# Scores of a differential attention as three 64-row products, two maps in the two halves of the array

## The chip, the cores and the metric

The kernel runs on one core of a Trainium2 chip. The metric is the device time of one execution in microseconds (us). Before the change it is 1723.46 us, the median of three runs (1720.41 to 1724.44).

## The reference: what is computed

One decoder layer over 2048 tokens of width 1024. A normalised input is projected once; half of the columns feed four heads of a gated delta rule, the other half four heads of differential attention; both outputs are concatenated and go through an output projection back to the residual stream. The change lies in the attention's scores. Each head has two maps `c`, with 64 columns of q and of k each:

```python
q = rmsnorm(q.reshape(b, t, DF_HEADS, 2, DF_HEAD_QK), q_gain) * (DF_HEAD_QK ** -0.5)
k = rmsnorm(k.reshape(b, t, DF_HEADS, 2, DF_HEAD_QK), k_gain)
...
s = jnp.einsum('bqhcd,bkhcd->bhcqk', q_blk, k).astype(jnp.float32)
mask = key_pos[None, :] <= q_pos[:, None]
p = jax.nn.softmax(jnp.where(mask, s, neg), axis=-1)
wts = p[:, :, 0] - lam * p[:, :, 1]
```

## The kernel before, in words

Products on TensorE use the rounded type `F32R`. Where more precision is wanted, a number is kept as a rounded part ("hi") and the rest ("lo"). So every q and k of the attention lies in DRAM twice, as hi and lo (`qst_d[h]`, `kst_d[h]`: 2 x 128 x 2048; the 128 are the 64 columns of map 0, then the 64 of map 1).

The program has two halves in time. The first 1100 us or so are the input projection (tiles `pnat`, `pct`) and the delta rule. Then, from about 1143 us to 1664 us, come the attention's scores, mixed with its values and with the output projection (`outp`). The attention goes through (head, group) pairs in the list `SEQ`: 4 heads x 8 groups of 256 query tokens, each group as two query blocks `qt` of 128. For each block, `scores` walks over the keys up to the diagonal in pieces of 512 (the last of 128 to 512), 160 pieces with two maps each in `m = 0, 1`:

- a PSUM bank `sp` is taken, one of three (`SPB = 3`);
- two products fill it, one with q-hi and one with q-lo as stationary matrix. `load_group` puts q twice into the 128 rows of `qs`, and `load_k` puts k-hi in rows 0 to 63 and k-lo in rows 64 to 127 of a tile per map. So one product of 128 rows gives q times (k-hi + k-lo);
- on the last piece a third product of 128 columns (`identr` and `cmask`) adds the causal mask;
- VectorE takes the row maximum (L940), ScalarE the exponential (L942) with it, and the bank is free again.

`values` then scales both maps, combines them (L994), transposes the weights on TensorE (`wtp`, evacuated at L1000 and L1002), and multiplies with v (`oT`, `pv`). `epilogue` normalises. `out_half` is the output projection.

TensorE works in program order. That order is set twice: by the generators (`abreast` interleaves scores, values and epilogue; `mingle` puts the output projection between), and then by the framework's scheduler, which reorders by its own estimate (`schedule_with_timeline_sim=True`). The `Recorder` class makes every product one source line: L113 (matmul) and L116 (transpose). Tiles tell them apart. The DMAs are issued on SyncE: k at L892, qs at L907.

In the changed file two lines stand ahead, so L113 is L115 there, L116 is L118, and so on.

One more product matters for the prediction. `ccp` at the start of the program transposes 60 rows of constants; it and the changed scores are the products that use 64 of the array's 128 rows as a tile of their own (the first transpose, `ngp`, uses 32, and `gctp` uses all rows and 32 columns).

Of the kernel before, what the change touches and what calls it, by code (L numbers as in the profile page):

```python
# [11 lines left out]
F32R = mybir.dt.float32r  # L12
# [4 lines left out]
P = 128  # L17
# [4 lines left out]
HALF = 1024  # L22
G = 512
# [25 lines left out]
QSB = 3  # L49
# [6 lines left out]
KB = (2, 2)  # L56
LAGX = 5
SPB = 3
# [5 lines left out]
WOR = 2  # L64
EXB = 14
WTB = 4

LEVELS = [1, 2, 4, 8, 16, 32, 64]

# [8 lines left out]
def f(ap):  # L78
    return ap.bitcast(F32)
# [3 lines left out]
def hybrid_kernel(  # L83
# [21 lines left out]
    V, A, PL, SY = nc.vector, nc.scalar, nc.gpsimd, nc.sync  # L105
# [55 lines left out]
    def bc(ap, shape):  # L161
        return ap.broadcast_to(shape)


    kst_d = [dram.tile([2, P, T], F32, name=f"kst_d{h}") for h in range(H)]
    qst_d = [dram.tile([2, P, T], F32, name=f"qst_d{h}") for h in range(H)]
# [708 lines left out]
    def bank(tag, name, bufs, shape=S4):  # L875
        return psa.tile(shape, F32, tag=tag, name=name, bufs=bufs)
# [8 lines left out]
    kst, vv = {}, {}  # L885

    def load_k(h, hf):
        cs = slice(hf * HALF, (hf + 1) * HALF)
        for m in range(2):
            k = kp.tile([P, HALF], F32R, tag=f"k{hf}", name=f"k{hf}", bufs=2 * KB[hf])  # L890
            for q in range(2):
                SY.dma_start(out=f(k[64 * q : 64 * q + 64]), in_=kst_d[h][q, 64 * m : 64 * m + 64, cs])  # L892
            kst[h, m, hf] = k

    def load_v(h, hf):
        cs = slice(hf * HALF, (hf + 1) * HALF)
# [4 lines left out]
    def load_group(h, g):  # L901
        c = dict(h=h, g=g, wt={})
        cs = slice(2 * g * P, 2 * (g + 1) * P)
        c["qs"] = qs = kp.tile([P, 2, 2, 2 * P], F32R, tag="qs", name="qs", bufs=QSB)
        for r in range(2):
            for m in range(2):
                SY.dma_start(  # L907
                    out=f(qs[64 * r : 64 * r + 64, m]),
                    in_=qst_d[h][:, 64 * m : 64 * m + 64, cs].rearrange("a p t -> p a t"),
                )  # L910
        c["zz"] = zz = kp.tile([P, 2 * P], F32, tag="azz", name="azz", bufs=QSB)
        SY.dma_start(out=zz, in_=z_d[h][:, cs])
        c["rs"] = kp.tile([P, 2, 2], F32, tag="rs", name="rs", bufs=5)
        return c

    def scores(c, qt):

        n = (2 * c["g"] + qt + 1) * P
        npc = (n + G - 1) // G
        nm = ap.tile([P, 2, 4], F32, tag="nm", name="nm", bufs=3)  # L920
        ss = ap.tile([P, 2, 4], F32, tag="ss", name="ss", bufs=3)
        c["ex"] = ex = {}
        for pi in range(npc):
            k0 = pi * G
            w = min(G, n - k0)
            for m in range(2):
                sp = bank("sp", "sp", SPB, [P, G])
                diag = pi == npc - 1
                for a in range(2):
                    PE.matmul(  # L930
                        sp[:, :w],
                        lhsT=c["qs"][:, m, a, qt * P : (qt + 1) * P],
                        rhs=kst[c["h"], m, k0 // HALF][:, k0 % HALF : k0 % HALF + w],
                        start=(a == 0),
                        stop=(a == 1 and not diag),
                    )
                if diag:
                    PE.matmul(sp[:, w - P : w], lhsT=identr, rhs=cmask, start=False, stop=True)
                mx = nm[:, m, pi : pi + 1]
                V.tensor_reduce(mx, sp[:, :w], axis=AX.X, op=ALU.max, negate=True)  # L940
                e = ap.tile([P, G], F32, tag="ex", name="ex", bufs=EXB)
                A.activation(e[:, :w], sp[:, :w], AF.Exp, bias=mx, accum_out=ss[:, m, pi : pi + 1])  # L942
                ex[m, pi] = e
                yield
        al = ap.tile([P, 2, 4], F32, tag="al", name="al", bufs=3)
        S3 = [P, 2, npc]
        if npc > 1:
            nmin = ap.tile([P, 2], F32, tag="nmin", name="nmin", bufs=3)
            V.tensor_reduce(nmin, nm[:, :, :npc], axis=AX.X, op=ALU.min)
            V.tensor_tensor(al[:, :, :npc], bc(nmin.unsqueeze(2), S3), nm[:, :, :npc], op=ALU.subtract)  # L950
            A.activation(al[:, :, :npc], al[:, :, :npc], AF.Exp)  # L951
        else:
            V.memset(al[:, :, 0:1], 1.0)
        c["al"], c["ss"] = al, ss
# [17 lines left out]
    def values(c, qt):  # L972
# [7 lines left out]
        for pi in range(npc):  # L980
            w = min(G, n - pi * G)
            nbk = w // P
            if pi not in wt:
                wt[pi] = ap.tile([P, 4, 2 * P], F32, tag="wt", name="wt", bufs=WTB)
            e0, e1 = ex[0, pi], ex[1, pi]
# [83 lines left out]
    def prefetch(i, j):  # L1069

        for n, (h, g) in enumerate(SEQ[:i]):
            for hf in range(g // 4 + 1):

                if n >= len(groups) and h not in have[hf][-KB[hf] :]:
                    have[hf].append(h)
                    load_k(h, hf)
                    if ap:
                        load_v(h, hf)
        for h, g in SEQ[len(groups) : j]:
            groups.append(load_group(h, g))  # L1080

    def attention():
        before = after = None
        for hf in range(2):
            for h in have[hf]:
                load_v(h, hf)
        for i in range(len(SEQ)):
            prefetch(i + 1, i + 1)
            prefetch(i + AHEAD, i + GA)
            for qt in range(2):  # L1090
                c = dict(groups[i])
                npc = (2 * c["g"] + qt + 4) // 4
                yield from abreast((scores(c, qt), 2 * npc), before, after)
                after = (epilogue(before[2]), 3) if before and qt == 0 else None
                before = (values(c, qt), (2 * npc + 1 if qt else npc + 1), c)
        scored[0] = True
        yield from abreast(before, after)
        yield from epilogue(before[2])
# [184 lines left out]
```

## Time and profile before

| | us |
|---|---|
| runs | 1720.41, 1723.46, 1724.44 |
| the profiled execution | 1718.26 |
| its span, first to last instruction | 1716.1 |
| TensorE busy in the span | 1622.8 (95%) |
| VectorE busy | 1066.1 (62%) |
| ScalarE busy | 751.6 (44%) |
| mean granted TensorE clock | 0.984 |

The profiled execution is 5.2 us under the median of the runs. Between its span and its time lie 2.2 us. A matmul's end in the trace is modelled; how fast TensorE goes through a row of products is read from the distance of their starts. "PEld" is the load of the stationary matrix, which normally runs beside the product before it.

### The profile page before, as it was taken

Reading aid. Unit: us, or ns where it says so; the run is one execution under the profiler, and the core shown is the slowest. Engines: PE = TensorE matmul, PEld = TensorE weight load, DVE = VectorE, ACT = ScalarE, POOL = GpSimd, SP = SyncE. Lnnn points to the kernel's source line nnn. Section 1 sums busy time; section 2 is a strip of 40 time slices with the busy share of each in tenths; the row PEclk is TensorE's granted clock in tenths of the full one; section 3 lists DMA queues with packets and bytes.
Section 4 is the critical chain, followed back from the end, with each engine's and each line's share of the span. In section 5 each row is a group of like instructions: output and inputs, shape, how many; then the busy total and the mean of one; then the engine's idle time right before and its main releaser. Section 6 shows DMA issues by size and latency. Waiting matters only on the chain.

```text
span 1716.1 us, 28068 instructions
## 1 busy us (share of the span) xinstructions
PE 1622.8 (95%) x9900; PEld 1414.1 (82%) x9900; DVE 1066.1 (62%) x2435; ACT 751.6 (44%) x2153; POOL 680.7 (40%) x789
## 2 busy tenths in 40 slices
PE   6999999999999899999999999989999989999987
PEld 5788899898988888889989898868777867778766
DVE  4765655645444486556573643337888778888772
ACT  5333333333334343433342333236777656565530
POOL 3454374253242256327344144022334354343432
PEclk9999999999999899999999999999999999999998
DMA  8232244233234341323313232596743364543343
GB/s 175 62 93 74 44 90 101 62 93 56 62 99 103 71 125 61 83 66 72 114 43 106 37 62 75 139 285 201 198 139 117 121 192 149 167 143 101 119 151 135
DMA packets 186969, 188.16 MB, mean 110 GB/s; under 512 B 12242, under 2 KB 142412, under 8 KB 186828
## 3 DMA queue, kind: packets, MB, share of 16 engines
q1 hardware_dynamic: 186556, 185.78, 39.5%
q8 instruction: 78, 1.28, 0.3%
q0 software_dynamic: 272, 0.59, 0.2%
q14 instruction: 63, 0.52, 0.1%
HBM read 124.42 MB, written 61.90 MB: 109 GB/s over the span
## 4 chain that ended last, share of the span: by engine, by line
PE 75%; DVE 8%; DMA 7%; ACT 4%; POOL 3%; issue 2%; SPq 1%; DVEq 0%; POOLq 0%; ACTq 0%
PE pct L113 24%; PE pnat L113 15%; PE outp L113 7%; PE oT L113 6%; PE sp L113 5%; PE wtp L116 2%; DVE nm L940 2%; PE xp L113 2%; DVE ex L994 2%; PE np L113 2%; PE tp L116 2%; DMA wr_fqk<-in_w_in_dram 2%; PE gqp L113 2%; ACT ex L942 1%; PE op L113 1%
## 5 line engine op out<-in xcount | busy, mean ns | idle before, releaser
L942 ACT ACTIVATE ex<-sp,nm 128x512 f32<-128x512 f32 (+3 forms) x320 | 198.5, 625 | 94.2 <-DVE nm L940 82.8
L113 PE MATMUL outp<-wo,mt 128*128 128x512 f32 x720 | 202.4, 414 | 5.2 <-ACT wo L1119 2.1
L940 DVE TENSOR_REDUCE nm<-sp 128x1 f32<-128x512 f32 (+3 forms) x320 | 186.3, 600 | 27.2 <-PE sp L113 25.6
L113 PE MATMUL sp<-k,qs 128*128 128x512 f32 (+3 forms) x640 | 184.4, 392 | 19.0 <-ACT ex L942 18.1
L113 PE MATMUL pnat<-wh_fqk,xh 128*128 128x256 f32 (+1 forms) x512 | 152.9, 300 | 16.0 <-ACT wh_fqk L336 8.8
L113 PEld LDWEIGHTS outp<-wo,mt 128*128 128x128 f32 x720 | 131.4, 193 | 31.4 <-ACT xr L1193 3.0
L113 PE MATMUL pnat<-wl_fqk,xh 128*128 128x256 f32 (+1 forms) x512 | 151.4, 297 | 1.6 <-POOL wl_fqk L337 1.6
L113 PE MATMUL pnat<-wh_fqk,xl 128*128 128x256 f32 (+1 forms) x512 | 150.1, 295 | 0.0
L113 PEld LDWEIGHTS sp<-k,qs 128*128 128x128 f32 x640 | 106.6, 190 | 49.6 <-ACT ex L942 37.5
L113 PE MATMUL oT<-wt,v 128*128 128x256 f32 (+1 forms) x576 | 132.7, 375 | 0.0
L528 DVE SCALAR_TENSOR_TENSOR cy<-craw,cc,cy 128x512 f32<-128x512 f32 x144 | 122.8, 853 | 3.3
L990 POOL TENSOR_SCALAR ex<-ex,al 128x512 f32<-128x512 f32 (+3 forms) x140 | 98.2, 716 | 61.4 <-ACT al L951 60.9
L113 PEld LDWEIGHTS oT<-wt,v 128*128 128x128 f32 x576 | 109.0, 193 | 16.2 <-ACT wt L1000 0.5
L994 DVE SCALAR_TENSOR_TENSOR ex<-ex,cf 128x512 f32<-128x512 f32 (+3 forms) x160 | 112.7, 743 | 12.9 <-ACT cf L969 10.0
L662 ACT CAST u_TT<-tp 128x512 fp32r<-128x512 f32 x112 | 65.5, 587 | 117.7 <-PE tp L116 117.6
L113 PEld LDWEIGHTS pnat<-wh_fqk,xh 128*128 128x128 f32 x512 | 99.7, 195 | 18.3 <-ACT wh_fqk L336 10.4
L113 PE MATMUL pct<-xh,wh_dvz 128*128 128x512 f32 x256 | 103.8, 406 | 0.0
L113 PE MATMUL pct<-xh,wh_dqk 128*128 128x512 f32 x256 | 103.5, 405 | 0.0
L113 PE MATMUL pct<-xl,wh_dvz 128*128 128x512 f32 x256 | 103.1, 403 | 0.0
L113 PE MATMUL pct<-xh,wl_dvz 128*128 128x512 f32 x256 | 103.0, 403 | 0.0
L113 PEld LDWEIGHTS pnat<-wl_fqk,xh 128*128 128x128 f32 x512 | 100.0, 195 | 3.3 <-POOL wl_fqk L337 3.0
L113 PE MATMUL pct<-xl,wh_dqk 128*128 128x512 f32 x256 | 102.6, 401 | 0.0
(271 smaller groups left out, 4179.4 us busy)
## 6 DMA issues: line engine op xcount, KB each, us to landing
qs<-qst_d SPq DMA_DIRECT2D x128, 128.0 KB, 3.1
mt<-mx_d SPq DMA_DIRECT2D x48, 256.0 KB, 4.0
k<-kst_d SPq DMA_DIRECT2D x40, 256.0 KB, 5.4
wr_dqk<-in_w_in_dram SPq DMA_DIRECT2D x32, 256.0 KB, 5.7
wr_dvz<-in_w_in_dram SPq DMA_DIRECT2D x32, 256.0 KB, 5.7
qst_d<-qkhl SPq DMA_DIRECT2D x16, 512.0 KB, 2.8
kst_d<-qkhl SPq DMA_DIRECT2D x16, 512.0 KB, 3.4
part_d<-xr SPq DMA_DIRECT2D x32, 256.0 KB, 3.7
```

What stands on the lines that cost most here:

```text
L113: last[0] = nc.tensor.matmul(*a, **k)
L116: last[0] = nc.tensor.transpose(*a, **k)
L528: V.scalar_tensor_tensor(y, raw[:, j : j + G], convc[:, j, idx : idx + 1], y, op0=ALU.mult, op1=ALU.add)
L662: A.copy(TT, f(tp))
L940: V.tensor_reduce(mx, sp[:, :w], axis=AX.X, op=ALU.max, negate=True)
L942: A.activation(e[:, :w], sp[:, :w], AF.Exp, bias=mx, accum_out=ss[:, m, pi : pi + 1])
L990: PL.tensor_scalar(e0[:, :w], e0[:, :w], al[:, 0, pi : pi + 1], 1.0, op0=ALU.mult, op1=ALU.mult)
L994: V.scalar_tensor_tensor(e1[:, :w], e1[:, :w], cf[:, pi : pi + 1], e0[:, :w], op0=ALU.mult, op1=ALU.add)
```

## The change

The scores' tiles hold q and k once, hi and lo side by side in the free dimension, with map 0 in rows 0 to 63 and map 1 in rows 64 to 127. For each piece two `sp` banks are taken together, and three terms (hi·hi, hi·lo, lo·hi; lo·lo is left out) are written as products of 64 rows, alternating between the maps. The mask, the maximum and the exponential follow for both maps. Four DMAs for k of a head's half become two, four for qs become one.

```diff
+TERMS = ((0, 0), (0, 1), (1, 0))
     def load_k(h, hf):
         cs = slice(hf * HALF, (hf + 1) * HALF)
-        for m in range(2):
-            k = kp.tile([P, HALF], F32R, tag=f"k{hf}", name=f"k{hf}", bufs=2 * KB[hf])
-            for q in range(2):
-                SY.dma_start(out=f(k[64 * q : 64 * q + 64]), in_=kst_d[h][q, 64 * m : 64 * m + 64, cs])
-            kst[h, m, hf] = k
+        k = kp.tile([P, 2, HALF], F32R, tag=f"k{hf}", name=f"k{hf}", bufs=KB[hf])
+        for q in range(2):
+            SY.dma_start(out=f(k[:, q]), in_=kst_d[h][q, :, cs])
+        kst[h, hf] = k
...
-        c["qs"] = qs = kp.tile([P, 2, 2, 2 * P], F32R, tag="qs", name="qs", bufs=QSB)
-        for r in range(2):
-            for m in range(2):
-                SY.dma_start(
-                    out=f(qs[64 * r : 64 * r + 64, m]),
-                    in_=qst_d[h][:, 64 * m : 64 * m + 64, cs].rearrange("a p t -> p a t"),
-                )
+        c["qs"] = qs = kp.tile([P, 2, 2 * P], F32R, tag="qs", name="qs", bufs=QSB)
+        SY.dma_start(out=f(qs), in_=qst_d[h][:, :, cs].rearrange("a p t -> p a t"))
...
-            for m in range(2):
-                sp = bank("sp", "sp", SPB, [P, G])
-                diag = pi == npc - 1
-                for a in range(2):
+            sps = [bank("sp", "sp", SPB, [P, G]) for m in range(2)]
+            diag = pi == npc - 1
+
+            for qa, ka in TERMS:
+                for m in range(2):
+                    rows = slice(64 * m, 64 * m + 64)
                     PE.matmul(
-                        sp[:, :w],
-                        lhsT=c["qs"][:, m, a, qt * P : (qt + 1) * P],
-                        rhs=kst[c["h"], m, k0 // HALF][:, k0 % HALF : k0 % HALF + w],
-                        start=(a == 0),
-                        stop=(a == 1 and not diag),
+                        sps[m][:, :w],
+                        lhsT=c["qs"][rows, qa, qt * P : (qt + 1) * P],
+                        rhs=kst[c["h"], k0 // HALF][rows, ka, k0 % HALF : k0 % HALF + w],
+                        start=(qa == 0 and ka == 0),
+                        stop=((qa, ka) == TERMS[-1] and not diag),
                     )
-                if diag:
+            if diag:
+                for sp in sps:
                     PE.matmul(sp[:, w - P : w], lhsT=identr, rhs=cmask, start=False, stop=True)
+            for m, sp in enumerate(sps):
                 mx = nm[:, m, pi : pi + 1]
```

The order of TensorE's instructions in the attention, before: the end of one query block of head 2 and the first pieces of the next (group 7, block 0, 512 keys a piece). The number behind `sp` is the bank's tile, so each number is one map of one piece; `x2` are its two products.

```order
L116 MATMUL wtp_15328<-ident_166,ex_15198 128x128 x4
L116 MATMUL wtp_15357<-ident_166,ex_15224 128x128
L113 MATMUL sp_15361<-k1_14324,qs_15098 128x256 x2
L113 MATMUL sp_15361<-cmask_11916,identr_171 128x128
L113 MATMUL sp_15386<-k0_13156,qs_15374 128x512 x2
L113 MATMUL sp_15408<-k0_13159,qs_15374 128x512 x2
L113 MATMUL sp_15424<-k0_13156,qs_15374 128x512 x2
L113 MATMUL sp_15434<-k0_13159,qs_15374 128x512 x2
L113 MATMUL sp_15448<-k1_14321,qs_15374 128x512 x2
```

The same place after the change: `sp_15444` and `sp_15445` are the two maps of the first piece, `sp_15484` and `sp_15485` those of the second.

```order
L115 MATMUL sp_15395<-cmask_11916,identr_171 128x128
L115 MATMUL outp_15366<-wo11_11959,mt_15216 128x512
L115 MATMUL sp_15444<-k0_13161,qs_15435 128x512 x3
L118 MATMUL aotp_15408<-ident_166,aon_15361 128x128 x2
L115 MATMUL outp_15366<-wo01_11958,mt_15216 128x512 x2
L115 MATMUL outp_15366<-wo11_11959,mt_15216 128x512
L115 MATMUL outp_15366<-wo01_11958,mt_15216 128x512
L115 MATMUL sp_15445<-k0_13161,qs_15435 128x512 x3
L115 MATMUL outp_15366<-wo01_11958,mt_15216 128x512
L115 MATMUL sp_15484<-k0_13161,qs_15435 128x512 x3
L115 MATMUL sp_15485<-k0_13161,qs_15435 128x512 x3
L118 MATMUL wtp_15464<-ident_166,ex_15315 128x128 x4
```

The six products of a piece, written in turn for the two maps, stand here as three of one map and then three of the other; in the first piece the two threes are apart, with other products of 128 rows between. Over the whole program the 960 products of 64 rows stand in 237 unbroken runs between instructions of 128 rows: 146 runs of three, 39 of six, 52 others. In 165 of the runs there is one map alone. Neighbours of different maps occur 149 times.

On SyncE's queue, at the start of the attention, the first head's k and the first two groups' q, before:

```order
L892 DMA k_11920<-kst_d_63 64x1024 x2
L892 DMA k_11923<-kst_d_63 64x1024 x2
L907 DMA qs<-qst_d_67 64x2x256 x4
L912 DMA azz<-z_d_73 128x256
L907 DMA qs<-qst_d_67 64x2x256 x4
```

and after:

```order
L893 DMA k_11920<-kst_d_63 128x1024 x2
L906 DMA qs<-qst_d_67 128x2x256
L908 DMA azz<-z_d_73 128x256
L906 DMA qs<-qst_d_67 128x2x256
L908 DMA azz<-z_d_73 128x256
```

The transfers stand in the same place; k takes half as many, twice as large, and qs one for four, with half the bytes.

## Rows read from the trace of the kernel before

**Rows 1.** The page: busy time of each engine over the span.
```profile
PE 1622.8 (95%) x9900; PEld 1414.1 (82%) x9900; DVE 1066.1 (62%) x2435; ACT 751.6 (44%) x2153; POOL 680.7 (40%) x789
```

**Rows 2.** Busy time by stretch, the attention: length, engines' us (instructions), clock, DMA share, GB/s.
```profile
1143.00:1664.00 521.00, 493.59 (x2590) 405.84 (x2588) 423.98 (x1058) 328.33 (x1046) 200.76 (x293) 0.99 0.51 155
```

**Rows 3.** The chain that ended last within the attention, shares by line.
```profile
by line: PE outp L113 19.1%; PE oT L113 16.8%; PE sp L113 15.6%; DVE nm L940 6.9%; PE wtp L116 6.8%; DVE ex L994 6.5%; ACT ex L942 4.8%; issue 3.6%; DMA out_dram<-xr 3.0%; DMA xr<-in_x_dram 2.7%; DVE wt L1002 1.4%; POOL ex L990 1.0%; POOL x
```

**Rows 4.** Groups by line and form, the scores' products: busy us, mean ns | idle before.
```profile
L113 PE MATMUL sp<-k,qs 128*128 128x512 f32 x448 | 142.9, 423 | 11.2 <-ACT ex L942 10.6
...
L113 PE MATMUL sp<-k,qs 128*128 128x384 f32 x64 | 18.4, 376 | 2.0 <-ACT ex L942 2.0
L113 PE MATMUL sp<-k,qs 128*128 128x256 f32 x64 | 13.7, 304 | 1.0 <-ACT ex L942 1.0
L113 PE MATMUL sp<-k,qs 128*128 128x128 f32 x64 | 12.4, 279 | 4.7 <-ACT ex L942 4.6
```

**Rows 5.** Timeline of TensorE at 1409 us: start, length (us), instruction, count.
```profile
1407.40 0.27 PE L116 MATMUL wtp<-ident,ex 128*128 128x128 f32 x1
...
1409.34 1.44 PE L113 MATMUL sp<-k,qs 128*128 128x512 f32 x6
1410.62 0.23 PE L113 MATMUL sp<-cmask,identr 128*128 128x128 f32 x1
...
1410.90 0.71 PE L116 MATMUL wtp<-ident,ex 128*128 128x128 f32 x5
```

**Rows 6.** The same six products by form, within 1409.30 to 1410.62.
```profile
L113 PE MATMUL sp<-k,qs 128*128 128x512 f32 x4 | 1.1, 394 | 0.0
L113 PE MATMUL sp<-k,qs 128*128 128x384 f32 x2 | 0.5, 338 | 0.0
```

**Rows 7.** Timeline of TensorE's products around `ccp`, the one of 60 rows.
```profile
28.61 0.29 PE L113 MATMUL pnat<-wl_fqk,xh 128*128 128x264 f32 x1
...
28.98 0.28 PE L113 MATMUL pnat<-wl_fqk,xh 128*128 128x264 f32 x1
29.10 0.28 PE L113 MATMUL pnat<-wh_fqk,xl 128*128 128x264 f32 x1
29.31 0.27 PE L116 MATMUL ccp<-ident,tmp 60*128 60x60 f32 x1
29.52 0.39 PE L113 MATMUL pnat<-wh_fqk,xh 128*128 128x264 f32 x1
29.74 0.29 PE L113 MATMUL pnat<-wl_fqk,xh 128*128 128x264 f32 x1
```

**Rows 8.** Timeline of the weight loads at the same place.
```profile
28.98 0.19 PEld L113 LDWEIGHTS pnat<-wh_fqk,xl 128*128 128x128 f32 x1
29.31 0.14 PEld L116 LDWEIGHTS ccp<-ident,tmp 60*128 60x128 f32 x1
29.51 0.19 PEld L113 LDWEIGHTS pnat<-wh_fqk,xh 128*128 128x128 f32 x1
29.62 0.19 PEld L113 LDWEIGHTS pnat<-wl_fqk,xh 128*128 128x128 f32 x1
```

**Rows 9.** Timeline of TensorE around `gctp`, 128 rows by 32 columns.
```profile
94.24 0.40 PE L113 MATMUL pct<-xl,wh_dvz 128*128 128x512 f32 x1
94.48 0.28 PE L116 MATMUL gctp<-ident,ts_gcl 128*32 128x128 f32 x1
...
94.82 0.39 PE L113 MATMUL pct<-xh,wh_dvz 128*128 128x512 f32 x1
```

**Rows 10.** Who waited for whom in the attention: us, times, longest.
```profile
PEld sp L113 <- ACT ex L942: 37.5, 63, 3.0
...
PE sp L113 <- ACT ex L942: 18.1, 35, 2.6
```

**Rows 11.** The page's DMA issues: count, KB each, us to landing.
```profile
qs<-qst_d SPq DMA_DIRECT2D x128, 128.0 KB, 3.1
...
k<-kst_d SPq DMA_DIRECT2D x40, 256.0 KB, 5.4
```

## The prediction

> **What bounds the kernel now.** I read the busy times first: TensorE is busy 95% of the span, the next engine, VectorE, 62% [rows 1]. The change touches only the attention, so the same view is taken of that stretch alone: of 521 us TensorE is busy 493.6, VectorE 424.0, ScalarE 328.3 [rows 2]. TensorE is idle for 27.4 us. The chain that ended last says the same: its largest shares are products, the scores' own 15.6%, and VectorE's and ScalarE's steps on the scores' banks (L940, L942, L994) follow far behind [rows 3]. So what TensorE gains or loses here mostly shows in the time, less what its waits give back.
>
> **What a product costs.** Lengths in the trace overlap; I take distances of starts. From 1409.34 to 1410.62 us six products of the scores start without a wait [rows 5], four of 512 columns and two of 384 [rows 6]: 1.28 us for 2816 columns, 0.4545 ns a column, or 0.233 us for 512. A weight load stays hidden: in a steady row the next one begins when the product before it does (28.98 against 28.98) [rows 7, 8].
>
> **Term 1, the columns.** Before: 448 x 512 + 64 x (384 + 256 + 128) = 278,528 columns [rows 4], about 127 us. The change makes three products for two, each on half of the rows. If the two maps always ran abreast, three product times would replace four: 208,896 columns, 69,632 fewer, a gain of 31.6 us. That is the price of the change as written. But the order that the scheduler made is another: three products of one map stand together, then three of the other, often with other work between. Products of one half can't run abreast with each other, since they use the same rows. One after another the 960 products are 417,792 columns: 139,264 more, **+63.3 us**. At the 149 places where a product follows one of the other map, the second could run beside the first. If all do, 56,832 columns are hidden and **+37.5 us** is left. No row shows two products abreast, and none excludes it; I take the middle, +50.
>
> The Trainium skill (TensorE: Matmul & The Clock Gate, Part 3 on packing small matmuls) says that products on different row groups run concurrently, some 4 ns apart. By that rule this term would be 37.5, and the forecast 12 us lower. No run here shows it.
>
> **Term 2, changing the shape of the array.** `ccp` is the one product of the trace that uses 64 of the rows as a tile and stands between products of 128. From the start of the last product before it (29.10) to that of the second one after it (29.74) are 0.64 us [rows 7]. Two products at their usual distance (28.61 to 29.10 are four: 0.122 each) make 0.245. `ccp` itself is at most a transposition of 128 columns, 0.11 us ((0.71 - 0.27) / 4) [rows 5]; for its 60 columns 0.05. So 0.285 to 0.34 us are left over, for going into the 64-row shape and out of it. The loads show how: ccp's begins at 29.31, 0.21 after the product before it, and the next at 29.51, 0.20 after ccp; the one after that, at 29.62, shows when the product's columns really start to flow [rows 8]. Where the shape changes, the load doesn't go ahead, so it is no longer hidden.
>
> The new program goes into that shape and out again 237 times (the runs that the order shows). At 0.285 this is 67.5 us, at 0.34 80.6; at nothing, if ccp stood there for a reason of its own, 0. I take 0.29, near the lower reading, since ccp had several waits to check first: **+69 us**.
>
> The Trainium skill (TensorEngine Tiling, Key Properties) has the rule: changing the tiling mode, not just the tile, drains TensorE. It gives no figure; the left-over at `ccp` agrees with it, the left-over at `gctp` doesn't (the rivals). It speaks against this change, which changes mode for every few products.
>
> **What is given back.** TensorE waits for a scores' bank today: the products stand idle 11.2 + 2.0 + 1.0 + 4.7 = 18.9 us [rows 4], nearly all behind ScalarE's exponential, and the weight loads 37.5 us for the same releaser [rows 10]. VectorE's and ScalarE's work stays as it is, 424 and 328 us, while TensorE's grows by over 100, so the banks will more often be free in time; and where TensorE still waits, a drain costs nothing. Against that, both banks of a piece are taken together out of three, and the first map's maximum can start only after three products. Between 0 and all 27.4 us of idle, I take **-25**.
>
> **The rest.** 96 DMAs for qs and 20 for k go, and qs moves half of its bytes [rows 11]. Their cover is the stretch before they are needed; the products wait for ScalarE and not for a transfer [rows 4], so nothing is gained. The mask's 128 products, maxima and exponentials stay; their place behind both maps delays VectorE, whose 424 us leave it time [rows 2] as long as TensorE is the slower. Leaving out lo·lo costs and saves nothing beyond term 1.
>
> **Sum.** 50 + 69 - 25 = +94 us on the profiled execution's 1718.3: 1812. The median of the runs is 5.2 us above that execution; I add them and say **1817 us**. With all ends of its terms (37.5 to 63.3, 67.5 to 80.6, 0 to 27.4 back) this case reaches from +78 to +144, 1801 to 1867 in the same measure. 0.2% of the time, 3.4 us, is what a measurement can tell from no change.
>
> **Rivals.**
> - *The shape costs nothing to change.* For it: `gctp` uses 32 columns of the array, and from the product before it to the second after it are 94.24 to 94.82, 0.58 us [rows 9], just 0.233 + 0.11 + 0.233. Against it: it is a tile of columns and not of rows, its load wasn't late, and ccp's was. Then only term 1 is left, +37.5 to +63.3, less 25: 1736 to 1762. Chance 0.18.
> - *Weights are exposed within the 64-row shape too.* The second and third product of a run have the same rows as the one before. If their load can't go ahead, each pays what a load exposes at ccp, 29.51 to 29.62, 0.11 us [rows 8]. 960 - 237 = 723 of them make 80 us more: about 1897. For products of 128 rows the loads do go ahead over the same rows [rows 8], which speaks against it. Chance 0.12. The Trainium skill (TensorE: Matmul & The Clock Gate, Part 3) does state that loads overlap with products only where the row group differs; the steady row's loads disagree with it.
> - *Faster, by the banks.* The change does do what it says where a run holds both maps, and the waits for banks go. If whole runs overlapped, half against half, 320,128 columns would be left, +18.9 us; with changes of shape free, all of the 27.4 us of idle gained makes it 8.5 us faster, 1715. It turns on the shape: from 8.5 / 237 = 0.036 us a run on, it is slower, and ccp showed eight times that. Chance 0.05; no change, between this and the first rival, 0.03.
> - *That the change does what it says throughout*, all maps abreast, is excluded by the order: 165 of 237 runs hold one map alone. The 31.6 us are what a program with the written order could look for.
>
> **How the numbers follow.** The forecast has 0.62, the first rival 0.18, the second 0.12, faster 0.05, no change 0.03. Slower by over 0.2%: 0.62 + 0.18 + 0.12 = 0.92; within 0.2%: 0.03; faster: 0.05. The range is the forecast's with the first rival's, 1740 to 1870; the dear weights, faster and no change stay out, together 0.20.
>
> **What would show it.** In the changed profile: the attention longer by about 90 us and everything before it as it was; 960 products of the scores with 64 rows; at each change of shape a weight load that begins 0.1 to 0.2 us late, and no such gap inside a run; starts 0.23 us apart within a run of one map and nearly together where the map changes; less waiting of the scores for L942. Products of 128 rows following a run at their usual distance would prove term 2 wrong and put the time near 1750. A gap before every product would mean the second rival. An attention no longer than 521 us would mean that the stretch wasn't bound by TensorE as I read it.

## The result, and the profile after

The changed kernel takes 1805.89 us, the median of four runs (1801.86 to 1815.44), against 1722.35 us before, now over four runs: a ratio of 1.0495 (95% interval 1.0469 to 1.052), 83.5 us slower. The profiled execution took 1808.26 us, with a span of 1806.6 us.

Busy time on the page of the changed kernel, against [rows 1]:

```profile
PE 1735.9 (96%) x10220; PEld 1440.1 (80%) x10220; DVE 1079.0 (60%) x2435; ACT 759.4 (42%) x2153; POOL 675.8 (37%) x789
```

The same view of two stretches of the changed kernel: everything before the attention, and the attention, from the first product of the scores to the last (length, busy us of TensorE, weight loads, VectorE, ScalarE, GpSimd, then clock, DMA share, GB/s).

```profile
0.00:1138.00 1138.00, 1091.84 (x7152) 978.49 (x7152) 627.75 (x1343) 417.83 (x1091) 466.60 (x481) 0.99 0.33 88
...
1138.00:1755.00 617.00, 607.49 (x2919) 433.22 (x2918) 431.66 (x1055) 335.65 (x1045) 195.43 (x295) 0.97 0.37 116
```

The attention begins 5 us earlier than before and takes 617 us instead of 521 [rows 2]. Inside it TensorE is idle for 9.5 us instead of 27.4, so its waits shrank, as foreseen. A second number moved that I had not looked at: the mean granted clock fell from 0.99 to 0.97.

The chain that ended last within the attention has far more of the scores' products than [rows 3], and less of the steps that free their banks:

```profile
by line: PE sp L115 32.9%; PE outp L115 21.0%; PE oT L115 17.4%; PE wtp L118 8.9%; DMA out_dram<-xr 3.2%; DVE nm L940 2.4%; DVE ex L994 2.2%; ACT ex L942 1.8%; PE aotp L118 1.4%; POOL ex L990 1.3%; DMA xr<-in_x_dram 1.2%; PE onp L118 1.2%;
```

The groups of the scores' products, against [rows 4], and the waits of their loads, against [rows 10]:

```profile
L115 PE MATMUL sp<-k,qs 64*128 64x512 f32 x672 | 173.2, 439 | 4.1 <-ACT ex L942 3.9
L115 PE MATMUL sp<-k,qs 64*128 64x384 f32 x96 | 26.3, 391 | 2.6 <-ACT ex L942 2.4
L115 PE MATMUL sp<-k,qs 64*128 64x256 f32 x96 | 19.2, 312 | 0.8 <-ACT ex L942 0.8
L115 PE MATMUL sp<-k,qs 64*128 64x128 f32 x96 | 16.4, 296 | 0.5 <-ACT ex L942 0.2
```
```profile
PEld sp L115 <- issue: 50.8, 183, 0.7
...
PEld sp L115 <- ACT ex L942: 21.9, 45, 1.3
```

The idle time before the products fell from 18.9 to 8.0 us. New is the first row of the waits: 183 loads that begin late although nothing in the profile holds them. Two runs on TensorE's timeline show what they are. Of six products of both maps, and of three of one map:

```profile
1408.19 0.97 PE L115 MATMUL sp<-k,qs 64*128 64x512 f32 x6
1409.09 0.92 PE L115 MATMUL oT<-wt,v 128*128 128x256 f32 x4
...
1414.13 0.66 PE L118 MATMUL wtp<-ident,ex 128*128 128x128 f32 x4
1414.72 0.97 PE L115 MATMUL sp<-k,qs 64*128 64x512 f32 x3
1415.61 0.55 PE L118 MATMUL wtp<-ident,ex 128*128 128x128 f32 x3
```

Six take 0.97 us, and three take 0.97 us. The six begin in pairs, at 1408.19, 1408.53 and 1408.76; the three begin singly, at 1414.72, 1415.06 and 1415.29. So two products on different halves do run abreast, at no cost here, and three alone leave half of the array unused. The loads around the second run:

```profile
1414.13 0.42 PEld L118 LDWEIGHTS wtp<-ident,ex 128*128 128x128 f32 x4 [0.36 <-ACT xr L1193]
1414.71 0.53 PEld L115 LDWEIGHTS sp<-k,qs 64*128 64x128 f32 x3 [0.17 <-ACT wo L1119]
1415.61 0.20 PEld L118 LDWEIGHTS wtp<-ident,ex 128*128 128x128 f32 x2 [0.37 <-issue]
```

At each border the load begins together with its own product (14.71 and 14.72; 15.61 and 15.61), not with the one before. That is the picture of `ccp` in [rows 8]. The first row of the waits counts 183 such loads ahead of scores' products; the changed kernel has 237 runs.

### The profile page after: what moved, and what is told of

Same layout as the page of the kernel before. It is cut to its first block, busy times and chain, and to the rows that moved or that the text cites. A ratio compares the mean times of both kernels' runs of the same rounds, so it can differ in the third digit from the quotient of the medians.

```text
span 1806.6 us, 28528 instructions
## 1 busy us (share of the span) xinstructions
PE 1735.9 (96%) x10220; PEld 1440.1 (80%) x10220; DVE 1079.0 (60%) x2435; ACT 759.4 (42%) x2153; POOL 675.8 (37%) x789
## 4 chain that ended last, share of the span: by engine, by line
PE 83%; DMA 5%; DVE 5%; POOL 2%; ACT 2%; issue 2%; SPq 0%; DVEq 0%; POOLq 0%; ACTq 0%
PE pct L115 23%; PE pnat L115 14%; PE sp L115 11%; PE outp L115 9%; PE oT L115 6%; PE wtp L118 3%; PE xp L115 2%; PE np L115 2%; PE tp L118 2%; PE gqp L115 1%; DMA wr_fqk<-in_w_in_dram 1%; PE op L115 1%; PE ysp L115 1%; DMA out_dram<-xr 1%; DMA u_gcr<-gc_d 1%
## 5 line engine op out<-in xcount | busy, mean ns | idle before, releaser
L115 PE MATMUL sp<-k,qs 64*128 64x512 f32 (+3 forms) x960 | 227.7, 407 | 8.0 <-ACT ex L942 7.2
L115 PE MATMUL outp<-wo,mt 128*128 128x512 f32 x720 | 212.8, 426 | 5.6 <-DVE xr L1171 2.5
L115 PEld LDWEIGHTS sp<-k,qs 64*128 64x128 f32 x960 | 126.6, 191 | 74.5 <-issue 29.4
L115 PE MATMUL oT<-wt,v 128*128 128x256 f32 (+1 forms) x576 | 137.0, 381 | 0.3 <-ACT wt L1000 0.2
L990 POOL TENSOR_SCALAR ex<-ex,al 128x512 f32<-128x512 f32 (+3 forms) x140 | 93.6, 684 | 110.9 <-ACT al L951 110.5
L115 PE MATMUL pct<-xh,wl_dqk 128*128 128x512 f32 x256 | 102.5, 404 | 0.0
```

Of the source, the lines that this page charges most:

```text
L115: last[0] = nc.tensor.matmul(*a, **k)
L990: PL.tensor_scalar(e0[:, :w], e0[:, :w], al[:, 0, pi : pi + 1], 1.0, op0=ALU.mult, op1=ALU.mult)
```

## The experiments

Nine kernels, each compared with runs of the kernel before on the same chip: 1720.93 us for the first four, 1720.95 for the next four, 1722.5 for the last. I name the theories as the expectations do: A is my forecast's, B its rival. The scheduler sets the order of each kernel anew, so two kernels can differ in more than the edit; where it matters, the text says so.

### The order as written, held on TensorE

```diff
+            for qa, ka, m in PIECE:
+                with tc.issue_after(prev) if prev else ExitStack():
                     PE.matmul(
...
+                if not prev and len(exps) > 1:
+                    tc.add_manual_dep(last[0].ins, exps[-2], BOTH, reason="both banks")
+                prev = last[0].ins
```

`PIECE` is the six terms in turn for the two maps; `exps` holds the exponentials, and `exps[-2]` is the one that frees the second map's bank.

> The changed kernel with the order that its text writes, held on TensorE: each first product of a piece also waits until the second map's bank is free, and the six products (and the masks) are chained, so 156 runs instead of 237, nearly all 0,1,0,1,0,1. Theory A (each run pays about 0.385 us for going into the 64-row shape and out; products of the two halves run abreast): columns 210,176 against 278,528 of before, 68,352 fewer at 0.4545 ns, -31 us; 156 x 0.385 = +60; less 0 to 25 us of waits given back: 1727 to 1751, about 1740. Theory B (the loss of the change is the serial order and the extra columns, the shape costs little): -31 us, 1700 or less, faster than before. If the halves did not run abreast at all: about +63 + 60, over 1800.

Measured: 1835.61 us, ratio 1.0673 (1.0647 to 1.0699). Slower than the change itself, and outside of what either theory gave. The expectation's last case, halves that do not run abreast at all, gave "over 1800" and would fit the time, but TensorE's timeline excludes it:

```profile
1314.22 0.96 PE L117 MATMUL sp<-k,qs 64*128 64x512 f32 x6
```

The halves do run abreast, yet the gain isn't there. Its attention, and who waited:

```profile
1134.00:1787.00 653.00, 560.78 (x2924) 405.36 (x2923) 440.64 (x1060) 332.13 (x1047) 203.52 (x300) 0.92 0.36 115
```
```profile
PEld sp L117 <- ACT ex L952: 85.3, 77, 2.4
```

TensorE is idle for 92.2 us (653 less 560.78), and the loads of the scores wait 85.3 us for the exponential, against 37.5 before [rows 10]. The granted clock is 0.92. This gave a second theory, A2: with three banks, taking two together leaves TensorE waiting, and in that stretch its clock is at the lower level more often.

### The same, by map

The edit is the order of `PIECE`: three products of map 0, then three of map 1.

> The same chaining and the same wait for both banks, but three products of map 0 and then three of map 1: 159 runs, nearly all 0,0,0,1,1,1, 345,984 columns if only the neighbours across the middle run abreast. Theory A: +31 us of columns and 159 x 0.385 = +61, less 0 to 25: 1789 to 1814, about 1795. Theory B: +31 less 25 at most: 1728 to 1753. Against the pairs kernel it has 135,808 columns more, 62 us, if the halves run abreast there, and the same time if they never do.

Measured: 1820.1 us, ratio 1.0583 (1.056 to 1.0606). The time is 6 us above theory A's range, and for another reason than it gave. It was to be 62 us slower than the pairs and is 15 us faster. TensorE's timeline of this kernel:

```profile
1303.25 0.96 PE L117 MATMUL sp<-k,qs 64*128 64x512 f32 x6 [0.43 <-ACT ex L952]
...
1309.00 0.97 PE L117 MATMUL sp<-k,qs 64*128 64x512 f32 x6
```

Six products take 0.96 us here too, though 143 of the 159 runs have them in the order 0,0,0,1,1,1. So TensorE begins the second map's products beside the first's in either order. What matters, as far as these runs show, is that both maps stand in one unbroken run. The attention:

```profile
1136.00:1770.00 634.00, 553.84 (x2929) 400.51 (x2928) 441.60 (x1061) 333.13 (x1047) 202.02 (x299) 0.93 0.37 118
```

Idle 80.2 us, clock 0.93: the same wait for two banks, a little shorter.

### One product of zeros, with 128 rows and with 64

```diff
+                PE.matmul(sp[:, :P], lhsT=nil, rhs=nil, start=False, stop=not diag)
```
```diff
+                PE.matmul(sp[:, :P], lhsT=nil[:64], rhs=nil[:64], start=False, stop=not diag)
```

Both are the kernel before with 320 small products added.

> The kernel before with one more product per map and piece (320), 128 rows and 128 columns of zeros added into the same bank. Both theories: 320 x 0.06 to 0.11 us = 19 to 35 us, less waits given back: 1722 to 1757, about 1738.

Measured: 1730.58 us, ratio 1.0063 (1.0039 to 1.0087), within what was expected.

> The same product of zeros with 64 rows instead of 128, in the same order: 320 lone changes of shape, nothing else. Theory A: 320 x 0.385 = 123 us over the kernel with 128 rows, of which up to 30 may fall into waits: 93 to 123 over it, about 1845. Theory B: the same time as with 128 rows, within 5 us. If a lone product costs what was read at ccp before (0.29): +93.

Measured: 1819.52 us, ratio 1.0586 (1.0562 to 1.061). The two kernels differ in nothing but the rows of the zeros (TensorE's order in the attention is the same in both), and by 88.9 us. Theory B falls: the shape's change costs 0.28 us per run, net. Theory A's 93 to 123 us is missed by 4: its 0.385 us a run was too much. The same place on TensorE's timeline, first with 128 rows:

```profile
1386.69 0.64 PE L113 MATMUL sp<-k,qs 128*128 128x512 f32 x2
1387.17 0.22 PE L113 MATMUL sp<-nil 128*128 128x128 f32 x1
1387.23 0.27 PE L113 MATMUL sp<-cmask,identr 128*128 128x128 f32 x1
1387.34 0.95 PE L116 MATMUL wtp<-ident,ex 128*128 128x128 f32 x7
1388.05 0.48 PE L113 MATMUL sp<-k,qs 128*128 128x512 f32 x1
```

then with 64:

```profile
1427.71 0.63 PE L113 MATMUL sp<-k,qs 128*128 128x512 f32 x2
1428.27 0.33 PE L113 MATMUL sp<-nil 64*128 64x128 f32 x1
1428.53 0.33 PE L113 MATMUL sp<-cmask,identr 128*128 128x128 f32 x1
1428.69 0.95 PE L116 MATMUL wtp<-ident,ex 128*128 128x128 f32 x7
1429.40 0.48 PE L113 MATMUL sp<-k,qs 128*128 128x512 f32 x1
```

From the scores' first product to the next piece's are 1.36 us, and 1.69: the detour costs 0.33 us here. It lies 0.08 ahead of the small product (0.48, 0.56), 0.20 behind it (0.06, 0.26) and 0.05 behind the next (0.11, 0.16). Sorted by the products before and behind, the places without a wait give a median difference of 0.34 us in nine groups of ten. `ccp` had shown 0.285 to 0.34 for the same; the upper reading was right. 320 x 0.33 is 106 us, and the kernel lost 89. The two attentions, 128 rows first:

```profile
1147.00:1682.00 535.00, 517.73 (x2903) 444.20 (x2902) 428.07 (x1058) 328.66 (x1044) 200.23 (x293) 0.99 0.52 152
```
```profile
1142.00:1770.00 628.00, 622.52 (x2908) 456.94 (x2906) 438.12 (x1059) 338.81 (x1048) 199.66 (x296) 0.98 0.43 130
```

With 64 rows TensorE is idle for 5.5 us instead of 17.3, and the attention begins 5 us earlier; together that is the 17 us between. The slightly lower clock is not in this sum.

### Three products of 128 rows per map

```diff
+                PE.matmul(sp[:, :w], lhsT=nil, rhs=kst[c["h"], m, k0 // HALF][:, k0 % HALF : k0 % HALF + w], start=False, stop=not diag)
```

> The kernel before with a third product of 128 rows per map and piece, zeros against the keys (the same columns as the serial count of the change, 417,792, no change of shape, the result as before). Both theories: 139,264 columns at 0.4545 ns = +63 us, less the 0 to 27 us of idle TensorE: 1757 to 1784, about 1762. If columns of the scores were hidden behind other engines, under 1740.

Measured: 1756.6 us, ratio 1.0191 (1.0165 to 1.0216): 35.7 us for 63.3 us of columns, just under the cheap end of what was expected (1757). Its attention:

```profile
1146.00:1705.00 559.00, 543.59 (x2893) 457.81 (x2892) 431.75 (x1058) 331.60 (x1047) 197.74 (x295) 0.99 0.48 142
```

15.4 us of idle are left, 12 fewer than before. 63.3 less 12 is 51 and not 36, so some 15 us more came back than show as idle. A product's end is modelled, so short waits may not show as idle; the scheduler's order is also another than before. No run separates the two. In this kernel a product more on TensorE cost about half of its length.

### The wait for both banks alone

The kernel before, its two products of 128 rows per map, with the chaining and the wait of the pairs.

> The kernel before, products of 128 rows, but with the chaining and the wait of the pairs kernel: the first product of a piece waits until the second map's bank is free too. Theory A2 (the pairs kernel lost its gain in the wait for two banks out of three, and in the lower clock that the idle array is granted): the pairs kernel is 115 us over before, of which -31 are columns and 156 x 0.28 to 0.39 = 44 to 61 changes of shape, so 85 to 102 us are left for wait and clock; with longer products somewhat less: 1780 to 1820. Theory B2 (runs with both maps are dearer than lone ones, the wait costs little): 1720 to 1740.

Measured: 1809.27 us, ratio 1.0506 (1.0484 to 1.0528). This lies in theory A2's range, and theory B2 falls: without a single product of 64 rows among the scores, taking both maps together with three banks costs 88 us. The edit brings the wait for the second bank, the chaining and, with them, another order by the scheduler; this run does not tell them apart. Its attention, and the wait of the scores' loads, twice the 37.5 us of [rows 10]:

```profile
1149.00:1756.00 607.00, 525.69 (x2590) 422.31 (x2589) 435.92 (x1061) 333.29 (x1046) 201.51 (x297) 0.94 0.46 137
```
```profile
PEld sp L114 <- ACT ex L954: 75.5, 69, 4.3
```

Idle 81.3 us against 27.4, clock 0.94 against 0.99, for the same 2590 products as in [rows 2].

### The pairs with four banks, and the control

```diff
-SPB = 3
-WTP = 2
+SPB = 4
+WTP = 1
```

In the pairs the wait is then for `exps[-3]`, which frees the second map's bank of four.

> The pairs kernel with four banks for scores and one instead of two for the transposed weights; 145 runs. Theory A2: the wait for two banks mostly goes, columns -31, runs +41 to +57, so 1731 to 1749 plus what the single bank of the transposes costs (the kernel before with the same banks tells that). Theory B2: as with three banks, 1830.

Measured: 1761.7 us, ratio 1.0223 (1.0192 to 1.0254), 74 us under the pairs with three banks. That is far from B2's 1830, but also above the 1731 to 1749 of theory A2, to which the control below adds 3.

> The kernel before with four banks for scores and one for the transposes, a control. The transposes' bank is evacuated in 0.7 us and then used again at once, so TensorE waits more for it and less for the scores: 1715 to 1790, no theory tells.

Measured: 1724.33 us, ratio 1.0019 (1.001 to 1.0029). The banks themselves cost next to nothing, and both pairs kernels are chained, so the 74 us are what the pairs lose by having three banks and not four: 52 us more of idle (92.2 against 40.6) and a lower clock (0.92 against 0.96). The pairs stay 37 us behind their control. Their attentions, the pairs' first:

```profile
1142.00:1686.00 544.00, 503.39 (x2823) 368.07 (x2822) 426.79 (x1049) 328.60 (x1038) 187.84 (x289) 0.96 0.40 126
```
```profile
1149.00:1648.00 499.00, 473.23 (x2497) 389.09 (x2495) 415.74 (x1050) 326.16 (x1038) 189.70 (x287) 0.99 0.52 153
```

The difference of 45 us, added up: about 68,000 columns fewer, -31; 145 runs at 0.33, +48; idle 40.6 against 25.8, +15; clock, 0.04 x 544 against 0.01 x 499, +17: +49. So in this kernel, even with nearly all of its columns saved, the shape costs more than it brings: a piece of 512 saves 0.233 us and pays 0.33. Idle and clock, which theory A2 took to be mostly gone, are the part that it missed.

### The change with four banks, order left to the scheduler

> The changed kernel itself, with four banks for scores and one for the transposes, the order left to the scheduler: 222 runs instead of 237, 146 of them still holding three or fewer products of one map. Theory A2: the scheduler splits the maps still, so the number of runs decides: runs 222 x 0.28 to 0.39 = 62 to 87, columns about +18 if the halves of a run flow abreast whatever their order, idle and clock as in the changed kernel: 1790 to 1815. If the third bank alone were what split the runs and cost the time: about as the pairs with four banks, 1762.

Measured: 1798.27 us, ratio 1.0423 (1.0373 to 1.0474), inside what A2 gave. A fourth bank alone doesn't mend the change: 222 runs are still there. Its attention:

```profile
1136.00:1717.00 581.00, 572.54 (x2821) 411.53 (x2820) 423.66 (x1049) 331.94 (x1038) 193.82 (x289) 0.97 0.38 119
```

The pairs with four banks are 37 us faster. By the expectations' counts (columns -31 there, +18 here) 49 us of that are columns and 25 us the 77 runs fewer, at 0.33; against it stand 32 us more of idle (40.6 against 8.5) and 4 us more of lost clock. That leaves 38.

None of these beats the kernel before.

## Why the prediction was right, and where its terms were off

The whole came out as said: slower, by 83.5 us against 94, in the attention, and most of it by the change of the array's shape. That the size came so near is in part luck: the columns were put at about twice what they cost, and a shape put too low, fewer waits given back and a clock that I had not looked at made up for it. Against the time before, the profiled execution of the change is 90 us longer:

| term | forecast | worked out from the runs |
|---|---|---|
| columns | +50 (37.5 to 63.3) | +19 to +26 |
| changes of shape, 237 | +69 (67.5 to 80.6) | +78 to +81 |
| waits given back | -25 (0 to -27.4) | -18 |
| granted clock | not foreseen | +15 |
| start of the attention | not foreseen | -5 |

The last column is worked out so: the columns by counting as abreast what the trace lets run abreast (below); the shape by 237 x 0.33 to 0.34 from the zeros; the idle by 27.4 - 9.5; the clock by half of the time that the traces' clock records put at 1.2 GHz, 41.0 us of the attention against 10.2 before; the start by the two first stretches. In the other kernels the attention begins between 1134 and 1149 us, and no run tells why. The terms add up to 89 to 99. The third product of 128 rows gave back some 15 us more than its idle showed, so an agreement this close does not prove each term.

**Columns, mis-sized.** I let products run abreast only where a product follows one of the other map, and set the middle between that and none. The halves are freer: in the runs shown that hold both maps, the shorter side is hidden whole, in either order. Counted so for all runs, that is 320,128 columns, 18.9 us, which the prediction used for its "faster" rival alone. By the starts in the trace it is some 335,000, 26 us: in the longest runs, of nine products and more, the later pieces run alone, in several of them after an idle gap. What I had right is that the scheduler's splitting of the maps turned a saving of 31.6 us into a loss: 165 runs with one map alone run with half of the array unused.

**Shape, right, and somewhat low.** The one `ccp` row carried it. I took the lower end of its reading; the zeros gave the upper, 0.33 us for in and out. The rule that changing the tiling mode drains TensorE (the Trainium skill, TensorEngine Tiling, Key Properties) agrees with these changes to 64 rows and back; the 0.58 us around `gctp` do not show it [rows 9].

**Given back, near the forecast.** 18 of the 27.4 us of idle went, against 25; what came back without showing as idle is not known for the change.

**The banks.** I wrote that both banks are taken together out of three, and set this against the shrinking waits. In the change it doesn't show: its threes take one bank at a time, and the idle before the scores fell to 8.0 us. Where the pairs are held together it is the largest cost of all: 88 us in the kernel before with wait and chaining, and 74 us between the pairs with three banks and with four. So with three banks the written order cost more here than the scheduler's.

**The clock.** Longer idle in an attention goes with a lower mean clock: 27.4 us with 0.99, 40.6 with 0.96, 81.3 with 0.94, 92.2 with 0.92. The two levels are 1.2 and 2.4 GHz, and the share that is lost adds to the wait: in the kernel before with wait and chaining, 67.7 us of the attention are at 1.2 GHz, of which half is lost, 29 us more than before; with 54 us more of idle that is 83 of its 86 us. But the change has only 9.5 us of idle and 0.97, and the lone zeros 5.5 us and 0.98. So idle isn't all of it. The longest stretch at 1.2 GHz in the changed attention begins at 1496.0, and the engine had not been idle before it:

```profile
1493.35 0.62 PE L115 MATMUL sp<-k,qs 64*128 64x256 f32 x3
1493.90 0.33 PE L115 MATMUL sp<-cmask,identr 128*128 128x128 f32 x1
1494.16 0.96 PE L115 MATMUL sp<-k,qs 64*128 64x512 f32 x3
1495.05 0.44 PE L118 MATMUL aotp<-ident,aon 128*128 128x128 f32 x2
1495.42 1.16 PE L115 MATMUL sp<-k,qs 64*128 64x512 f32 x3
```
```profile
1496.00:1513.00 17.00, 16.60 (x47) 11.17 (x45) 11.12 (x26) 7.86 (x23) 7.02 (x10) 0.50 0.22 74
```

Here threes of one half stand ahead of the fall, with the other half of the array unused. Whether these lower the clock stays open; no run was made for it.

**The rivals.** That the shape costs nothing fell with the zeros. That weights are exposed within a run fell too: in the run of three shown above, from the first start (1414.72) to the load behind the run (1415.61) are 0.89 us, which is one exposed load of 0.11, three products of 0.233 and the 0.08 of a border; two more exposed loads have no room. "Faster by the banks" failed on its own condition, 0.036 us a run against 0.33.

## What to carry to other kernels

Before splitting an array by rows, count the unbroken runs that the final order has, not the loops of the source: each cost about 0.33 us here to enter and leave, and only what both halves held in the same run was done twice as fast. A piece of 512 columns saved 0.233 us, so a run of one piece could not pay. By these two numbers, as an estimate, it would have to hold two; no run here shows that it pays then. And holding two operations together also holds their buffers together: check that the banks for both are free before the engine needs them.

## What the runs showed of the hardware that I had not expected

- TensorE takes up the second half's products beside the first's even when three of the first stand ahead in its order: six in 0.96 us in the kernel ordered by map. So "TensorE works in program order", as said at the start, does not hold between the two halves.
- Entering the 64-row shape cost a late load on each side even around a product of 128 columns of zeros; but a tile of 32 columns (`gctp`) had cost nothing [rows 9]. As far as one row can tell, not every change of shape has this cost.
- The granted clock of the attention fell from 0.99 to 0.94 in a kernel whose products are those of before, in another order and with three times the idle time on TensorE; the lower level's share cost about 29 us more there, beside 54 of idle.
